# Strassen's scheme for up-projection pairs 2 to 18 in a one-core decoder layer

## The chip, the cores and the metric

The kernel runs on one core of a Trainium2 chip. The metric is the device time of one execution in microseconds (us). A run gives one time; the kernel before has three, and one further execution was taken with the hardware profiler, whose trace is read here. The core has a matrix engine (TensorE, PE in the profile, with its weight loads as PEld), VectorE (DVE), ScalarE (ACT), GpSimd (POOL) and SyncE (SP); SP and POOL here mostly issue DMAs.

## The reference

One layer of a decoder trunk on x of 512 positions by 1024 channels, float32. The changed part is the second half, the ConvGLU:

```python
h = rms_norm(x, g_ffn)
u = causal_depthwise_conv(h @ w_up, conv_w, conv_b)      # w_up: 1024 x 5632, conv of width 3
u_gate, u_val = split(u, 2)                              # 2816 columns each
x = x + (silu(u_gate) * u_val) @ w_down                  # w_down: 2816 x 1024
return rms_norm(x, g_final)
```

Ahead of it stand an RMS norm, the input projection, two attention branches of 8 heads, their gated merge (`g * (y @ W)` for two branches) and the output projection `m @ w_out` with the residual.

## The kernel before, in words

All products are done in the single-pass fp32r format with each operand split in a high part (a ScalarE copy to fp32r) and a low part (VectorE: value minus high part). One product is three matmuls, high by high, high by low, low by high (`mm3`, lines 90 to 92). Weights come from HBM into a raw tile of 128x1024 (five buffers, `wraw`), and the two parts go to rotating tiles, three for high parts and three for low parts (`wtile`).

The order of the PE instructions is the program's order. On the other engines a planner orders the instructions by a simulated time line, within the dependences and the explicit `issue_after` constraints, which say that an instruction stands behind another one.

The stages, in time order: input projection and attention; then the merge loop (`for i in range(KT)`), which for each of 8 blocks of 128 channels takes the gate projections from block 3 on and the two branch products with weight `ab`; the output projection, in Strassen form over 2x2 blocks; the residual, norm and transposes (`x1_root`, `x1_scale`, `x1_turn`, `x1_out`), which give `h2`, the normed activations, transposed, as 8 tiles of 128 channels by 512 positions in two parts; then the up-projection; then the down-projection, again in Strassen form, and the final norm.

The up-projection goes over 22 pairs. Pair i is columns 128i to 128i+127 of the gate half and of the value half of `w_up`. A plain pair (`plain`) takes two products of 1024 channels with 512 positions, 2 x 8 x 3 = 48 matmuls of 512 columns. The first two pairs, 0 and 1, are computed ahead in halves of 256 positions (`up_half`), the second half of the positions first, while the first half of the positions is still being transposed. A mixed pair treats the 2x2 blocks (channel half, gate or value) times (channel half, position half) by Strassen's scheme in seven block products of 4 x 3 = 12 matmuls of 256 columns, 84 in all (`first_four` has 48 of them: X, Q, Y, Z; `last_three` has 36). `MIXED` names the mixed pairs, 4 to 19. The PE order is first_four(i), last_three(i-1), first_four(i+1), and so on.

A mixed pair needs three things besides the plain ones:

- Sums of weights, made early by DMAs with addition between DRAM tensors (`sums_of`, tile `usum`, on POOL's DMA queue): per pair one copy of 1 MB, one addition of 512 KB and two additions of 256 KB.
- Split weights: `wa` (raw weights), `wb` and `wc` (sums), `wd` (half a tile), by `wmix`. For `wc` the low parts were computed during the merge loop (`split_ahead`: load the sum as `praw`, ACT and DVE split it, store the low part to DRAM as `ulo`) and are only loaded by SP (`wlo<-ulo`).
- Sums of activations (`mixes`): the four quadrants of `h2` in plain float32 are put into `h32` (two tiles, shown as `xa` in the trace) by 8 DMAs that copy the high parts and 8 DMAs that add the low parts (lines 1031 and 1033, POOL's queue); `mixes` makes four sums of 128x1024 on DVE (lines 965 to 968), and splits each with one ACT and one DVE instruction (lines 970 and 971) into `tm4`. `tm4[0]`, used by Y, is the first one that PE needs, then `tm4[2]` by Z, `tm4[1]` and `tm4[3]` by last_three.

After its products every pair goes through `glu`: the width-3 convolution (two ACT and four DVE instructions, lines 911 to 914), SiLU on ACT (917), the product (928), and after odd pairs the sums for the down-projection (576 to 579) and their split (337 and 338).

`step` (lines 665 and 666) makes a one-element copy on DVE and one on POOL, behind which the next part of a list of DMAs is issued; three such steps in `glu` belong to the weight sums of the down-projection (`dsums`).

Of the kernel before, what the change touches and what calls it, by code (L numbers as in the profile page):

```python
# [10 lines left out]
F32 = mybir.dt.float32  # L11
F32R = mybir.dt.float32r
# [15 lines left out]
NP = FT // 2  # L28
MIXED = range(4, 20)
SPILL = (1, 2, 3)  # L30
HOMES = (8, 10, 7)
DSUM = (0, 4, 5)
AHEAD = MIXED
NL = 3
# [12 lines left out]
def trunk_layer(ctx: ExitStack, tc: tile.TileContext, x: bass.AP, xT: bass.AP, w: bass.AP, vec: bass.AP,  # L47
# [223 lines left out]
    with tc.issue_after(nc.gpsimd.tensor_copy(small[:, 31:], r1[:, :1]).ins):  # L271
        for _ in quarter_sums("oi", list(enumerate(osum))):
            pass
        usum = {i: wdr.tile([4, 128, 512], F32, name=f"usum{i}") for i in MIXED}

        def sums_of(pairs, n=3):
            for group in (pairs[j:j + n] for j in range(0, len(pairs), n)):
                for i in group:
                    nc.gpsimd.dma_start(usum[i], flat(("ui", i, 0), 2), max_dma_last_dim=8192)
                for i in group:  # L280
                    adds(usum[i][0:2], flat(("ui", i, 2), 1))
                for i in group:
                    adds(usum[i][3], usum[i][0])
                for i in group:
                    adds(usum[i][2], usum[i][3])

        sums_of(MIXED)

# [301 lines left out]
    psp = pool(tst, "psp", 1)  # L590
    ulo = {i: wdr.tile([128, 2, 512], F32R, name=f"ulo{i}") for i in AHEAD}
    ahead = list(AHEAD)

    def both(q):
        return q.rearrange("h p c -> p h c")

    def split_ahead():
        if not ahead:
            return
        i = ahead.pop(0)  # L600
        raw = psp.tile([128, 2, 512], F32, name="praw", bufs=3)
        nc.gpsimd.dma_start(raw, both(usum[i][2:4]))
        with tc.issue_after(wload.hi.ins):
            nc.scalar.activation(phi, raw, AF.Copy)
        lo = raw.bitcast(F32R)
        with tc.issue_after(wload.lo.ins):
            nc.vector.tensor_sub(lo, raw, phi.bitcast(F32))
        nc.gpsimd.dma_start(ulo[i], lo)

    for i in range(KT):  # L610
        if i >= NG:
            fillers.append(gates(i, split_ahead))
            fill(1000)
        wab = wload(("ab", i))
        split_ahead()
        g = pend[i]
        for b, br in enumerate("ab"):
            ps = pmm.tile([128, S], F32, name="mm")
            for p in range(4):
                mm3(ps, blk(wab, b * 4 + p), (yhl[br, p][:, 0], yhl[br, p][:, 1]), p == 0, p == 3)  # L620
# [18 lines left out]
    x1s = pool(hst, "x1s", 1, side="right")  # L639
    h2 = [x1s.tile([128, 2, S], F32R, name=f"h2{k}") for k in range(KT)]  # L640
    ost = ExitStack()
# [14 lines left out]
    splits = []  # L656
    dsums = (step for q in dsum.items() for step in quarter_sums("di", [q]))
    marks = iter(list(range(16, 31)) + list(range(8)))

    def step(todo, src):  # L660
        c = next(marks, None)
        if c is None:
            return
        seen = small[:, c:c + 1]
        nc.vector.tensor_copy(seen, src)
        with tc.issue_after(nc.gpsimd.tensor_copy(seen, seen).ins):
            next(todo, None)

    def split_in(p, raw):
# [213 lines left out]
    up_half(ups[3], wup[3], 1)  # L883
    for n in range(4):
        up_half(ups[n], wup[n], 0)
# [20 lines left out]
    def glu(i, us):  # L906
# [17 lines left out]
        elif i // 2 not in xa:  # L924
            j = i // 2
            xa[j] = xtile(j if j < 7 else SPILL[j - 7] if j < NP - 1 else 9)
        j = i // 2
        split = a_side(i % 2, lambda dst: nc.vector.tensor_mul(dst, ua, ub), glu.tm, xa[j] if i % 2 else None, xb[j])
        if split and i >= FT - 3:
            return split  # L930
        if split:
            split()
            if j in SPILL:
# [4 lines left out]
                for h in range(2):  # L938
                    nc.gpsimd.dma_start(away["a", j][:, h], xa[j][:, h])
        if i < 3:  # L940
            step(dsums, xb[j][:, 0, :1] if i % 2 else glu.tm[:, 0, :1])
        return split
# [18 lines left out]
    def mixes():  # L961
        neg = cw[:, :, FT + MIXED[0]:FT + MIXED[-1] + 1]
        nc.vector.tensor_scalar(neg, neg, -1.0, None, op0=OP.mult)
        b11, b12, b21, b22 = (quad(h, T) for h in range(2) for T in range(2))
        nc.vector.tensor_sub(b11, b11, b12)
        nc.vector.tensor_sub(b12, b22, b12)
        nc.vector.scalar_tensor_tensor(b22, b11, -1.0, b22, op0=OP.mult, op1=OP.subtract)
        nc.vector.scalar_tensor_tensor(b21, b22, -1.0, b21, op0=OP.mult, op1=OP.subtract)
        for n, q in enumerate((b11, b22, b12, b21)):
            nc.scalar.activation(tm4[n][:, 0], q, AF.Copy)  # L970
            nc.vector.tensor_sub(tm4[n][:, 1], q, tm4[n][:, 0].bitcast(F32))

# [10 lines left out]
    def wmix(i, parts, n=1024, lo=None):  # L983
# [11 lines left out]
        return hi, wlo  # L995

    def first_four(i):
        wa = wmix(i, [(slice(0, 1024), w[WIDX["up", i, 0]])])
        wb = wmix(i, [(None, both(usum[i][0:2]))])
        ps1, ps2 = up_ps(), up_ps()  # L1000
        X, Q, Y, Z = ps1[:, :256], ps1[:, 256:], ps2[:, :256], ps2[:, 256:]
        quarter(X, wa, 0, rows_of(0, 0), True)
        quarter(Q, wa, 1, rows_of(1, 0), False)
        quarter(Y, wb, 1, mixed_rows(1), True)
        quarter(Z, wb, 0, mixed_rows(3), False)
        p1s, p5s, v = (tmp[i % 2][:, n] for n in range(3))
        nc.scalar.activation(p1s, X, AF.Copy)
        nc.scalar.activation(p5s, Y, AF.Copy)
        nc.vector.tensor_add(v, Z, p5s)
        return ps1, ps2, p1s, v  # L1010

    def last_three(i, ps1, ps2, p1s, v):
        X, Q, Y, Z = ps1[:, :256], ps1[:, 256:], ps2[:, :256], ps2[:, 256:]
        wc = wmix(i, [(None, both(usum[i][2:4]))], lo=ulo.get(i))
        wd = wmix(i, [(slice(0, 512), w[WIDX["up", i, 1]][:, 512:])], 512)
# [11 lines left out]

    for i in range(2):
        plain(i)
    for k in range(KT):  # L1030
        nc.gpsimd.dma_start(h32[k // 4][:, k % 4], h2[k][:, 0].bitcast(F32))
    for k in range(KT):
        nc.gpsimd.dma_start(h32[k // 4][:, k % 4], h2[k][:, 1].bitcast(F32), accum_op=OP.add)
    for i in range(2, MIXED[0]):
        if i == MIXED[0] - 1:
            mixes()
        plain(i)
    prev = None
    for i in MIXED:
        cur = i, *first_four(i)  # L1040
        if prev:
            last_three(*prev)
        prev = cur
# [229 lines left out]
```

## Time and profile before

| | |
|---|---|
| three runs | 701.58, 702.32, 702.64 us; median 702.32 us |
| the profiled execution | 701.36 us, of which 699.6 us are the span from the first to the last instruction |
| PE busy | 690.9 us (99%), 4460 matmuls |
| PEld / DVE / ACT / POOL busy | 604.3 / 573.7 / 404.3 / 123.8 us |
| DMA | 184.13 MB, 263 GB/s on average |

Times inside the trace count from the span's start. A matmul's row shows its start and a length that includes the pipeline's depth; so the distance of two starts is what a matmul costs, not its length. A line number is that of the kernel before.

### The profile page before, as it was taken

To read this page: it belongs to the slowest core of one execution; us is meant where nothing else is said; L and a number is where in the kernel's file an instruction comes from. 1 tells how busy PE (TensorE), PEld (TensorE's weight loads), DVE (VectorE), ACT (ScalarE), POOL (GpSimd) and SP (SyncE) were. 2 spreads that over 40 slices of the span, in tenths; PEclk is the share of its full clock that TensorE was granted. 3 is DMA by queue.
4 is the path that set the end of the run, shared out by engine and by line. 5 is a ranking of instruction groups with operands and counts; after the bars stand their busy time and mean duration, and the time that the engine had idled before them with its cause. 6 is when DMAs were issued, how large, how long until landed. Compare 5 with 4: busy or idle time off the path is not lost.

```text
span 699.6 us, 11729 instructions
## 1 busy us (share of the span) xinstructions
PE 690.9 (99%) x4460; PEld 604.3 (86%) x4460; DVE 573.7 (82%) x901; ACT 404.3 (58%) x607; POOL 123.8 (18%) x200
## 2 busy tenths in 40 slices
PE   9999999999999999999999999999999999999995
PEld 6888888979888888888889889999999988888884
DVE  7778858598694777586876899989999998878996
ACT  6435445455564455445576666777777764546854
POOL 1211122233542122112312410000000003200000
PEclk9999999999999999999999999999999999999999
DMA  8799999999999688787998968889777765867703
GB/s 313 277 339 368 358 353 238 240 237 246 228 266 291 230 294 273 270 270 273 350 340 290 208 176 300 291 306 326 250 240 250 261 220 199 311 209 249 265 0 121
DMA packets 57577, 184.13 MB, mean 263 GB/s; under 512 B 6640, under 2 KB 7408, under 8 KB 51632
## 3 DMA queue, kind: packets, MB, share of 16 engines
q1 hardware_dynamic: 41136, 105.18, 42.5%
q0 software_dynamic: 16096, 77.87, 39.8%
q8 instruction: 35, 0.57, 0.3%
q10 hardware_dynamic: 288, 0.33, 0.1%
q14 instruction: 22, 0.18, 0.1%
HBM read 162.64 MB, written 64.75 MB: 325 GB/s over the span
## 4 chain that ended last, share of the span: by engine, by line
PE 98%; DVE 1%; ACT 1%; DMA 1%; issue 0%; ACTq 0%
PE b L92 12%; PE b L90 12%; PE b L91 12%; PE mm L90 11%; PE mm L92 11%; PE mm L91 11%; PE c L91 5%; PE c L90 5%; PE c L92 5%; PE q L209 3%; PE tp L480 3%; PE tp L504 3%; PE sc L404 1%; PE sc L414 1%; PE v L91 1%; PE v L90 1%
## 5 line engine op out<-in xcount | busy, mean ns | idle before, releaser
L90 PE MATMUL b<-h,whi 128*128 128x256 f32 (+1 forms) x320 | 95.8, 299 | 0.0
L91 PE MATMUL b<-h,whi 128*128 128x256 f32 (+1 forms) x320 | 95.7, 299 | 0.0
L92 PE MATMUL b<-h,wlo 128*128 128x256 f32 (+1 forms) x320 | 95.7, 299 | 0.0
L90 PE MATMUL mm<-xg,whi 128*128 128x512 f32 x224 | 89.8, 401 | 0.0
L85 ACT ACTIVATE whi<-raw 128x1024 fp32r<-128x1024 f32 (+2 forms) x62 | 59.8, 975 | 51.4 <-PE mm L92 16.8
L92 PE MATMUL mm<-xg,wlo 128*128 128x512 f32 x224 | 87.4, 390 | 0.0
L91 PE MATMUL mm<-xg,whi 128*128 128x512 f32 x224 | 87.3, 390 | 0.0
L992 ACT ACTIVATE whi<-raw 128x1024 fp32r<-128x1024 f32 x64 | 61.1, 954 | 37.5 <-PE b L91 28.1
L86 DVE TENSOR_TENSOR wlo<-raw,whi 128x1024 fp32r<-128x1024 f32 (+2 forms) x62 | 68.6, 1115 | 12.9 <-ACT whi L85 12.6
L90 PE MATMUL b<-xa,whi 128*128 128x256 f32 x256 | 70.7, 276 | 0.0
L91 PE MATMUL b<-xa,whi 128*128 128x256 f32 x256 | 70.7, 276 | 0.0
L672 ACT ACTIVATE whi<-raw 128x1024 fp32r<-128x1024 f32 x45 | 46.8, 1052 | 31.9 <-DVE raw L690 11.8
L90 PEld LDWEIGHTS b<-h,whi 128*128 128x128 f32 x320 | 60.1, 188 | 2.5
L91 PEld LDWEIGHTS b<-h,whi 128*128 128x128 f32 x320 | 60.1, 188 | 2.5
L92 PEld LDWEIGHTS b<-h,wlo 128*128 128x128 f32 x320 | 60.1, 188 | 2.5
L672 DVE TENSOR_TENSOR wlo<-raw,whi 128x1024 fp32r<-128x1024 f32 x45 | 54.7, 1221 | 5.7 <-ACT whi L672 5.6
L92 PE MATMUL b<-xa,wlo 128*128 128x256 f32 x192 | 53.0, 276 | 0.0
L90 PEld LDWEIGHTS mm<-xg,whi 128*128 128x128 f32 x224 | 42.1, 188 | 9.9 <-issue 1.8
L92 PEld LDWEIGHTS mm<-xg,wlo 128*128 128x128 f32 x224 | 42.0, 188 | 9.0
L91 PEld LDWEIGHTS mm<-xg,whi 128*128 128x128 f32 x224 | 42.2, 188 | 7.9
L91 PEld LDWEIGHTS b<-xa,whi 128*128 128x128 f32 x256 | 48.1, 188 | 0.0
L90 PEld LDWEIGHTS b<-xa,whi 128*128 128x128 f32 x256 | 48.1, 188 | 0.0
(282 smaller groups left out, 1747.4 us busy)
## 6 DMA issues: line engine op xcount, KB each, us to landing
raw<-w SPq DMA_DIRECT2D x103, 512.0 KB, 5.8
usum<-w POOLq DMA_DIRECT2D x16, 1024.0 KB, 25.6
raw<-usum SPq DMA_DIRECT2D x32, 512.0 KB, 5.2
usum<-w POOLq DMA_DIRECT2D x16, 512.0 KB, 19.6
usum<-usum POOLq DMA_DIRECT2D x32, 256.0 KB, 12.0
praw<-usum POOLq DMA_DIRECT2D x16, 512.0 KB, 5.6
ulo<-praw POOLq DMA_DIRECT2D x16, 512.0 KB, 5.3
wlo<-ulo SPq DMA_DIRECT2D x32, 256.0 KB, 3.6
```

The lines of the kernel that those rows point to most:

```text
L85: wload.hi = nc.scalar.activation(hi[:, sl], raw[:, sl], AF.Copy)
L86: wload.lo = nc.vector.tensor_sub(lo[:, sl], raw[:, sl], hi[:, sl].bitcast(F32))
L90: nc.tensor.matmul(ps, a[0], b[0], start=start, stop=False, **kw)
L91: nc.tensor.matmul(ps, a[0], b[1], start=False, stop=False, **kw)
L92: nc.tensor.matmul(ps, a[1], b[0], start=False, stop=stop, **kw)
L209: nc.tensor.matmul(qk0[c], w0[i][:, (k % 2) * 512 + c * 128:(k % 2) * 512 + (c + 1) * 128], xg[k][:, j], start=(k == 0 and n == 0), stop=( ...
L404: nc.tensor.matmul(scs[h // 2][:, h % 2, o:o + n], Q[i][r0:r0 + 32, c, qt * 128:(qt + 1) * 128], K[i][r0:r0 + 32, d, :n], start=False, sto ...
L414: nc.tensor.matmul(sc[:, h, o:o + n], q[r0:r0 + 64, c, qt * 128:(qt + 1) * 128], k[r0:r0 + 64, d, :n], start=m == 0, stop=m == 2, skip_gro ...
L480: nc.tensor.transpose(tp[:, h, c:c + 128], a[:, h, c:c + 128], ident)
L504: nc.tensor.matmul(av[h * 64:(h + 1) * 64, j, qt * 128:(qt + 1) * 128], v[:, kb, (2 * p + h) * 64:(2 * p + h + 1) * 64], aT[p][:, h, o + k ...
L672: splits.append((nc.scalar.activation(hi, raw, AF.Copy), nc.vector.tensor_sub(lo, raw, hi.bitcast(F32))))
L992: nc.scalar.activation(hi[:, :n], raw[:, :n], AF.Copy)
```

## The change

- `MIXED` goes from pairs 4 to 19 to pairs 2 to 18: 17 mixed pairs, and five plain ones (0, 1, 19, 20, 21).
- `AHEAD`, the low parts computed in the merge loop, goes from `wc` of all 16 mixed pairs to `wc` of pairs 2 to 15 and `wb` of pairs 2 and 3, 16 pieces again. For pairs 16 to 18 `wc` is split by DVE when it is used. In the merge loop the pieces begin at block 1, not at block 0.
- `h32` no longer comes from DMAs. For the first half of the positions 8 ACT copies take it from the transposes' PSUM banks; for the second half two DVE additions of 128x1024 join the parts of `h2`, which is one tile now.
- `mixes` becomes a generator in the order `tm4[2]`, `tm4[0]`, `tm4[1]`, `tm4[3]`; signs are moved into the splits. The first `wa`'s split is put behind the first of these splits, `first_four(2)`'s copy of X and all of `first_four(3)` behind the second, the two remaining plain `glu`s (pairs 0 and 1) behind the third and the fourth.
- The four halves of `up_half` for the first positions go in the order 2, 0, 1, 3, not 0, 1, 2, 3.
- The three `dsums` steps stand before the sums of `glu`, and `sums_of` has become a generator that is run to its end at once.

```diff
-MIXED = range(4, 20)
+MIXED = range(2, 19)
-AHEAD = MIXED
+AHEAD = sorted([(i, 1) for i in MIXED[:14]] + [(i, 0) for i in MIXED[:2]], key=lambda q: (q[0], -q[1]))
...
-    ulo = {i: wdr.tile([128, 2, 512], F32R, name=f"ulo{i}") for i in AHEAD}
+    ulo = {(i, h): wdr.tile([128, 2, 512], F32R, name=f"ulo{i}{h}") for i, h in AHEAD}
...
         wab = wload(("ab", i))
-        split_ahead()
+        if i:
+            split_ahead()
...
-    for n in range(4):
+    for n in (2, 0, 1, 3):
         up_half(ups[n], wup[n], 0)
...
-        nc.vector.tensor_sub(b11, b11, b12)
-        nc.vector.tensor_sub(b12, b22, b12)
-        nc.vector.scalar_tensor_tensor(b22, b11, -1.0, b22, op0=OP.mult, op1=OP.subtract)
-        nc.vector.scalar_tensor_tensor(b21, b22, -1.0, b21, op0=OP.mult, op1=OP.subtract)
-        for n, q in enumerate((b11, b22, b12, b21)):
-            nc.scalar.activation(tm4[n][:, 0], q, AF.Copy)
-            nc.vector.tensor_sub(tm4[n][:, 1], q, tm4[n][:, 0].bitcast(F32))
+        def halve(n, q, sign=1.0):
+            hi, lo = tm4[n][:, 0], tm4[n][:, 1]
+            act = nc.scalar.activation(hi, q, AF.Copy, scale=sign)
+            return act.ins, nc.vector.scalar_tensor_tensor(lo, q, sign, hi.bitcast(F32), op0=OP.mult, op1=OP.subtract).ins
+
+        nc.vector.tensor_sub(b22, b22, b12)
+        yield halve(2, b22)
+        nc.vector.tensor_sub(b12, b11, b12)
+        yield halve(0, b12)
+        nc.vector.tensor_add(b11, b11, b22)
+        yield halve(1, b11, -1.0)
+        nc.vector.tensor_sub(b21, b11, b21)
+        yield halve(3, b21)
...
-        wa = wmix(i, [(slice(0, 1024), w[WIDX["up", i, 0]])])
-        wb = wmix(i, [(None, both(usum[i][0:2]))])
+        with behind(early if i == MIXED[0] else ()):
+            wa = wmix(i, [(slice(0, 1024), w[WIDX["up", i, 0]])])
+            wb = wmix(i, [(None, both(usum[i][0:2]))], lo=ulo.get((i, 0)))
...
-    for i in range(2):
-        plain(i)
-    for k in range(KT):
-        nc.gpsimd.dma_start(h32[k // 4][:, k % 4], h2[k][:, 0].bitcast(F32))
-    for k in range(KT):
-        nc.gpsimd.dma_start(h32[k // 4][:, k % 4], h2[k][:, 1].bitcast(F32), accum_op=OP.add)
-    for i in range(2, MIXED[0]):
-        if i == MIXED[0] - 1:
-            mixes()
-        plain(i)
+    for k in (0, 2, 1, 3, 4, 6, 5, 7):
+        src = turn_banks[0, k // 4][k % 4 // 2][:, k % 2 * 256:(k % 2 + 1) * 256]
+        nc.scalar.activation(h32[k // 4][:, k % 4, :256], src, AF.Copy, scale=gffn[:, k:k + 1])
+    for h in range(2):
+        nc.vector.tensor_add(quad(h, 1), *(h2all[:, 4 * h:4 * h + 4, c, 256:].bitcast(F32) for c in range(2)))
+    mixed_in = mixes()
+    early = next(mixed_in)
+    ready = next(mixed_in)
+    for i in range(MIXED[0]):
+        with behind(next(mixed_in, ())):
+            plain(i)
     prev = None
     for i in MIXED:
-        cur = i, *first_four(i)
+        with behind(ready if i == MIXED[0] + 1 else ()):
+            cur = i, *first_four(i)
```

More of the change, by code (lines that the diff above doesn't have):

```diff
@@ L279, in sums_of @@
                     nc.gpsimd.dma_start(usum[i], flat(("ui", i, 0), 2), max_dma_last_dim=8192)
+                yield
                 for i in group:
                     adds(usum[i][0:2], flat(("ui", i, 2), 1))
+                yield
                 for i in group:
                     adds(usum[i][3], usum[i][0])
+                yield
                 for i in group:
                     adds(usum[i][2], usum[i][3])
-        sums_of(MIXED)
+                yield
+        for _ in sums_of(MIXED):
+            pass
     mqkp = pool(ysta, "mqkp", 4, side="right")
@@ L595, in both, with step @@
         return q.rearrange("h p c -> p h c")
+    dsums = (step for q in dsum.items() for step in quarter_sums("di", [q]))
+    marks = iter(list(range(16, 31)) + list(range(8)))
+    def step(todo, src):
+        c = next(marks, None)
+        if c is None:
+            return
+        seen = small[:, c:c + 1]
+        nc.vector.tensor_copy(seen, src)
+        with tc.issue_after(nc.gpsimd.tensor_copy(seen, seen).ins):
+            next(todo, None)
     def split_ahead():
@@ L599, in split_ahead @@
             return
-        i = ahead.pop(0)
+        q = i, h = ahead.pop(0)
         raw = psp.tile([128, 2, 512], F32, name="praw", bufs=3)
-        nc.gpsimd.dma_start(raw, both(usum[i][2:4]))
+        nc.gpsimd.dma_start(raw, both(usum[i][2 * h:2 * h + 2]))
         with tc.issue_after(wload.hi.ins):
@@ L607, in split_ahead @@
             nc.vector.tensor_sub(lo, raw, phi.bitcast(F32))
-        nc.gpsimd.dma_start(ulo[i], lo)
+        nc.gpsimd.dma_start(ulo[q], lo)
     for i in range(KT):
@@ L639, in trunk_layer @@
     x1s = pool(hst, "x1s", 1, side="right")
-    h2 = [x1s.tile([128, 2, S], F32R, name=f"h2{k}") for k in range(KT)]
+    h2all = x1s.tile([128, KT, 2, S], F32R, name="h2")
+    h2 = [h2all[:, k] for k in range(KT)]
     ost = ExitStack()
@@ L656, in trunk_layer @@
     splits = []
[L657 to L667, printed above, removed]
     def split_in(p, raw):
@@ L927, in glu @@
         j = i // 2
+        if i < 3:
+            step(dsums, uc[0][:, :1])
         split = a_side(i % 2, lambda dst: nc.vector.tensor_mul(dst, ua, ub), glu.tm, xa[j] if i % 2 else None, xb[j])
@@ L939, in glu @@
                     nc.gpsimd.dma_start(away["a", j][:, h], xa[j][:, h])
-        if i < 3:
-            step(dsums, xb[j][:, 0, :1] if i % 2 else glu.tm[:, 0, :1])
         return split
@@ L995, in wmix, with behind @@
         return hi, wlo
+    def behind(ins):
+        st = ExitStack()
+        for q in ins:
+            st.enter_context(tc.issue_after(q))
+        return st
     def first_four(i):
-        wa = wmix(i, [(slice(0, 1024), w[WIDX["up", i, 0]])])
-        wb = wmix(i, [(None, both(usum[i][0:2]))])
+        with behind(early if i == MIXED[0] else ()):
+            wa = wmix(i, [(slice(0, 1024), w[WIDX["up", i, 0]])])
+            wb = wmix(i, [(None, both(usum[i][0:2]))], lo=ulo.get((i, 0)))
         ps1, ps2 = up_ps(), up_ps()
@@ L1006, in first_four @@
         p1s, p5s, v = (tmp[i % 2][:, n] for n in range(3))
-        nc.scalar.activation(p1s, X, AF.Copy)
+        with behind(ready if i == MIXED[0] else ()):
+            nc.scalar.activation(p1s, X, AF.Copy)
         nc.scalar.activation(p5s, Y, AF.Copy)
@@ L1013, in last_three @@
         X, Q, Y, Z = ps1[:, :256], ps1[:, 256:], ps2[:, :256], ps2[:, 256:]
-        wc = wmix(i, [(None, both(usum[i][2:4]))], lo=ulo.get(i))
+        wc = wmix(i, [(None, both(usum[i][2:4]))], lo=ulo.get((i, 1)))
         wd = wmix(i, [(slice(0, 512), w[WIDX["up", i, 1]][:, 512:])], 512)
```

## The prediction

> **What bounds the kernel now.** I read the page first: busy times, the 40 slices, the chain that ended last.
>
> ```profile
> span 699.6 us, 11729 instructions
> PE 690.9 (99%) x4460; PEld 604.3 (86%) x4460; DVE 573.7 (82%) x901; ACT 404.3 (58%) x607; POOL 123.8 (18%) x200
> PE   9999999999999999999999999999999999999995
> DVE  7778858598694777586876899989999998878996
> PEclk9999999999999999999999999999999999999999
> PE 98%; DVE 1%; ACT 1%; DMA 1%; issue 0%; ACTq 0%
> ```
>
> PE carries 98% of the chain at the full clock. DVE stands at nine tenths through the last third of the slices, where the mixed pairs are, so it is the engine that can become late next. A busy PE is not yet a dense one, so next came starts of matmuls at the borders of the up-projection, and the windows between them.
>
> ```profile
> 391.20 0.40 PE L90 MATMUL b<-h,whi 128*128 128x512 f32 x1
> 412.98 0.28 PE L90 MATMUL b<-h,whi 128*128 128x256 f32 x1
> 565.31 0.40 PE L90 MATMUL b<-h,whi 128*128 128x512 f32 x1
> ...
> 391.20:412.98 21.78, 21.78 (x98) 18.02 (x97) 19.58 (x30) 12.91 (x15) 6.75 (x10) 1.00 0.93 209
> 412.98:565.31 152.33, 152.33 (x1345) 152.32 (x1344) 144.94 (x226) 112.30 (x169) 4.39 (x8) 1.00 0.79 272
> 565.31:587.10 21.79, 21.79 (x99) 18.02 (x97) 20.46 (x33) 11.70 (x16) 2.85 (x5) 1.00 0.50 167
> ```
>
> In a window stand its length, then busy time and instructions of PE, PEld, DVE, ACT, POOL, the clock, the DMA share and GB/s. The first and the last window are two plain pairs each, the middle one the 16 mixed pairs. By the code a plain pair has 48 matmuls and a mixed pair 84 (counts here take in one or two that overlap a border). 21.78 / 96 = 226.9 ns per 512 columns, 152.33 / 1344 = 113.3 ns per 256: half to within 0.1 ns, so no stall hides in either stage. A plain pair is 10.89 us, a mixed one 9.52 us.
>
> **The change, part by part.** *One plain pair becomes mixed (17, not 16):* 10.89 - 9.52 = 1.37 us less on PE, which sets the end. This is the one sure term, since no stall is there to be removed.
>
> *The start of the mixed stage* moves ahead by two pairs. Pairs 0 and 1 have been computed in halves, so PE goes from the last half straight into X of pair 2, where it now begins pair 2 as a plain one, at 391.20. X and Q take 24 x 113.3 ns = 2.72 us, so Y needs `tm4[0]` at 393.92, Z needs `tm4[2]` at 395.28, the next X comes at 396.64 and last_three(2) at 402.08. What stands before that:
>
> ```profile
> 379.08 0.86 ACT L807 ACTIVATE h<-b,vecs 128x256 fp32r<-128x256 f32 x2 [0.21 <-DVE h L808]
> 382.96 1.06 ACT L85 ACTIVATE whi<-raw 128x1024 fp32r<-128x1024 f32 x1 [3.02 <-PE b L91]
> 385.68 1.06 ACT L85 ACTIVATE whi<-raw 128x1024 fp32r<-128x1024 f32 x1 [1.66 <-PE b L91]
> ...
> 375.54 1.23 DVE L828 TENSOR_TENSOR wlo<-raw,whi 128x1024 fp32r<-128x1024 f32 x1 [1.43 <-ACT whi L824]
> 379.58 0.88 DVE L808 SCALAR_TENSOR_TENSOR h<-b,vecs,h 128x256 fp32r<-128x256 f32 x2 [0.15 <-ACT h L807]
> 384.06 1.23 DVE L86 TENSOR_TENSOR wlo<-raw,whi 128x1024 fp32r<-128x1024 f32 x1 [3.59 <-ACT whi L85]
> 404.31 1.22 DVE L965 TENSOR_TENSOR xa<-xa 128x1024 f32<-128x1024 f32 x1
> 405.45 0.74 DVE L912 SCALAR_TENSOR_TENSOR t<-b,vecs,t 128x511 f32<-128x511 f32 x1
> ...
> L971 DVE TENSOR_TENSOR xa<-xa,xa x4: 1212/1214/1218, 406.9 to 420.7; 128x1024 fp32r<-128x1024 f32 x4
> L807 ACT ACTIVATE h<-b,vecs x16: 457/474/477, 364.8 to 379.5; 128x256 fp32r<-128x256 f32 x16
> 380.50:391.20 10.70, 10.70 (x96) 10.70 (x94) 5.65 (x7) 4.24 (x5) 5.07 (x7) 1.00 1.03 299
> ```
>
> ACT and DVE end the transposes' output at 379.94 and 380.46 and then idle 3.02 and 3.59 us; in the 10.7 us to 391.2 they work 4.24 and 5.65. The new chain goes there. ACT: eight copies of the form of line 807, 8 x 0.474 = 3.8 us, four of which are needed first. DVE: two additions, four sums and four low parts of 128x1024, ten of 1.22 us, 1.14 apart when dense (404.31 to 405.45), so 11.4 us; ACT's four high parts of 1.06 lie between. To Y go two additions, two sums, two low parts; with the low part of `wa` for pair 2 behind them that is seven: 380.46 + 7 x 1.14 = 388.4, 2.8 us before 391.20. The weight tile for this `wa` is free in time: before, the first two halves' weight tiles come free at 382.96 and 385.68 (what ACT waits for there), in the order 2, 0, 1, 3 one half later, 385.68 and about 388.4. If all ten and `wa` go first, PE waits: 380.46 + 11 x 1.22 = 393.9, 2.7 us late. Below nothing is excluded, as PE is dense from 377 on. I take 0, since the constraint behind the first split is what puts `wa` early; the end 2.7 stays for the range. The addition of the second half can begin earlier still, in the 1.43 us of idle before 375.54.
>
> The `glu` of pairs 0 and 1, behind the third and fourth split, is late by this, but its PSUM banks are wanted only by pair 4, at 406.2: nothing.
>
> *Low parts for `wb` of pairs 2 and 3 by DMA, `wc` of 16 to 18 on DVE.* The loads wait for a weight tile and stand in order on SP; raw loads behind them were issued pairs ahead.
>
> ```profile
> L991 SPq DMA_DIRECT2D wlo<-ulo x32: 320/415/1259, 418.6 to 555.3; - x32
> DMA to landing us min/median/max: 2.5/3.6/5.5
> 425.00:555.00 130.00, 130.00 (x1150) 130.00 (x1148) 123.91 (x196) 95.14 (x143) 4.39 (x8) 1.00 0.81 279
> L994 DVE TENSOR_TENSOR wlo<-raw,whi 128x1024 fp32r<-128x1024 f32 x28 | 34.1, 1217 | 1.3 <-ACT whi L992 1.3
> ```
>
> `wb` of pair 2 has a tile from 388.4 and is needed at 393.9, `wb` of 3 from 393.9 to 399.4, `wc` of 2 from 396.6 to 402.1: 5.5 us each, with a landing of 3.6 in the median and 5.5 at worst. Cost 0, at worst some 0.5 for the second issue; without this cover DVE would pay 1.22 a piece. On DVE a mixed pair costs 123.91 / 130 x 9.52 = 9.07 us of 9.52. Pairs 16 to 18 add 1.22: 10.3, 0.77 too much, 2.3 us behind after three. Pair i's PSUM sums have to be done only before last_three(i+2), 15 us after its own end, and then three plain pairs follow, not two, each with 48 matmuls to hide `glu` in. So 0; price without that cover, 2.3.
>
> *The POOL queue.* Four more DMAs for the 17th pair stand ahead of the first `praw`; 16 DMAs of `h32` go.
>
> ```profile
> 29.59 2.25 POOL L251 DMA_DIRECT2D osum<-w  x4
> 212.76 0.76 POOL L246 DMA_DIRECT2D usum<-usum  x1 [1.03 <-DMA usum<-usum]
> 214.22 0.77 POOL L602 DMA_DIRECT2D praw<-usum  x1 [0.70 <-DVE g L536]
> DMA to landing us min/median/max: 2.9/5.4/12.8
> 231.01 1.01 ACT L604 ACTIVATE spare<-praw 128x1024 fp32r<-128x1024 f32 x1
> 240.29 0.39 PE L90 MATMUL mm<-ya,whi 128*128 128x512 f32 x1
> ...
> 377.05 0.54 POOL L1031 DMA_DIRECT2D xa<-h  x1 [10.97 <-ACT h L807]
> 397.35 2.95 POOL L1033 DMA_DIRECT2D xa<-h  x3
> ```
>
> The 80 DMAs of both sums (5 x 16, 64 of `usum`, 16 of `osum`) take 29.59 to 212.76, 2.29 us each, so `praw` moves by 9.2, to land at 214.22 + 9.2 + 12.8 = 236.2. Beginning at block 1 moves its first use by one step of 24 matmuls, 5.44 us, to 236.45. What is queued behind it on ACT and DVE is the split of block 2's `ab` weights, needed by PE at 240.29: 236.2 + 1.0 + 1.06 + 1.22 = 239.5. Taken as 0; by the same row's median the load is 7 us early, and at worst a further 2 us of queueing would cost about 1.2. The last piece lies in slot 16 of 17, not of 18; the tiles that follow into its memory are wanted much later. `h32`'s DMAs, first row to last in the fence, gave DMA a share of 1.03 at 380 to 391; gone, they help SP's loads, and PE not at all. The moved `dsums` steps are as many as before: 0.
>
> **Sum.** 701.36 - 1.37 = 699.99 for the profiled execution, which stands 0.96 under the runs' median; on the median, 702.32 - 1.37 = 700.95. About 0.2% (1.4 us) is what a measurement of this kernel can tell from no change, and the forecast lies almost on that border.
>
> **The rivals.**
>
> A, *the start is late* (the other side): the first `wa` or `tm4[0]` comes after PE. It decides from 2.8 us of delay in the chain above, that is if the planner puts third and fourth split, or a `glu`, ahead of it. Price 2.7: 702.32 - 1.37 + 2.7 = 703.65; a convolution of pair 0 ahead of it as well, four instructions of 0.74, makes it 5.7 late, 706.6. Against it: the slack, and no PE stall in a stage where DVE is 95% busy.
>
> B, *DVE or a queue runs out of cover*, at pairs 16 to 18 (up to 2.3) or at the first `praw` (up to 1.2): 701.3 to 703.3.
>
> C, *more matmuls cost by their number*: a fixed part in each would eat into the saving, 36 of them. The two spacings above leave room for 0.1 ns each, 0.00 us; this has a chance of 0.03 for other tiles. The Trainium skill, "TensorE: Matmul & The Clock Gate", section "Wait — 56ns, not 53.3ns?", gives about 2.5 ns for each warm matmul on top of its columns; with that a mixed pair would be 84 x (2.5 + 112.2) = 9.63, the saving 1.26 and the time 701.06. By that rule the two spacings would differ from 2:1 by 2.5 ns; this trace has 0.1 and does not agree.
>
> D, *small delays go too*: PE has 0.37 us of lateness at the start of the down-projection,
>
> ```profile
> 591.63 0.39 PE L92 MATMUL c<-whi,xa 128*128 128x512 f32 x1
> 592.05 0.47 PE L90 MATMUL c<-whi,xa 128*128 128x512 f32 x1
> 592.36 0.40 PE L91 MATMUL c<-wlo,xa 128*128 128x512 f32 x1
> 603.94 0.49 PE L91 MATMUL c<-wlo,xa 128*128 128x512 f32 x1
> 604.27 0.40 PE L92 MATMUL c<-whi,xa 128*128 128x512 f32 x1
> ```
>
> three spacings of 0.42, 0.31 and 0.33 against 0.227. With three plain pairs ahead DVE may be on time there: 700.6.
>
> **How the numbers follow.** The forecast, 1.37 kept, 0.57 (own range 700.4 to 701.5: half of the three runs' spread of 1.06 us on either side); half of it falls beyond the border. D 0.13, faster. C 0.03, same. A 0.16: 0.13 slower, and 0.03 same where the lateness is about what PE saves. B 0.11, half of it same and half slower. So faster 0.42, same 0.40, slower 0.18. Range 700.2 to 703.5: D's lower end with the same spread, up to the nearer end of A; beyond lie A's worse part and little else.
>
> **What would show it.** After: 17 x 84 matmuls of 256 columns from about 391.2 to 553.1 without a wait, three plain pairs to 585.7, then the down-projection 1.37 us earlier. Wrong would be: PE idle before Y of pair 2 with DVE at `tm4`, idle near 240 with ACT at `praw`, or spacings over 113.3 ns in pairs 16 to 18.

## The result, and the profile after

| | before | after |
|---|---|---|
| median (22 runs each) | 702.27 us | 706.12 us |
| the profiled execution | 701.36 us, span 699.6 us | 702.12 us, span 700.4 us |

The ratio is 1.0053 (95% interval 1.0042 to 1.0063): the change makes the kernel 3.8 us slower, where 1.4 us of gain were forecast. One of the 22 runs of the kernel before, of 771.33 us, was in a slow state and does not count in the ratio (without it the median is 702.25). The changed kernel's time spreads from 701.79 to 709.24 us, and its profiled execution is among the quickest, so a second execution, of 706.39 us, is read beside it below ("the second execution").

The page of the changed kernel, the lines that answer to those of before:

```profile
span 700.4 us, 11800 instructions
PE 691.2 (99%) x4496; PEld 605.0 (86%) x4496; DVE 578.3 (83%) x909; ACT 409.0 (58%) x620; POOL 112.9 (16%) x188
...
PE   9999999999999999999999999999999999999995
...
PEclk9999999999999999999999999999999999999999
...
PE 95%; DVE 2%; DMA 1%; ACT 1%; issue 1%; ACTq 0%; DVEq 0%
```

There are 36 matmuls more, as there must be, and PE is still at 95% of the chain. The stages tell more. First the windows of the kernel before, from the first gate product of the merge loop on: merge loop, first half of the output projection, the halves of pairs 0 and 1, and pair 2 to the down-projection.

```profile
225.20:327.33 102.13, 102.13 (x452) 84.59 (x451) 72.72 (x89) 48.47 (x53) 19.75 (x33) 1.00 0.80 265
327.33:349.09 21.76, 21.76 (x97) 18.02 (x96) 19.35 (x33) 12.51 (x16) 8.88 (x16) 1.00 1.02 360
367.19:391.20 24.01, 24.01 (x210) 24.01 (x208) 16.57 (x33) 14.41 (x29) 7.80 (x12) 1.00 0.87 277
391.20:587.10 195.90, 195.90 (x1539) 188.38 (x1537) 184.98 (x287) 136.91 (x198) 13.98 (x23) 1.00 0.77 253
```

The same stages of the changed kernel, with the mixed pairs (392.88 to 554.72) by themselves as well:

```profile
225.54:327.68 102.14, 102.14 (x453) 84.60 (x452) 70.90 (x88) 47.68 (x53) 21.13 (x35) 1.00 0.82 268
327.68:349.65 21.97, 21.97 (x97) 17.94 (x96) 18.13 (x30) 12.21 (x15) 7.99 (x15) 1.00 1.00 370
368.62:392.88 24.26, 24.26 (x209) 24.25 (x208) 21.77 (x36) 19.11 (x40) 0.56 (x1) 1.00 0.50 184
392.88:587.47 194.59, 194.59 (x1575) 188.79 (x1573) 185.74 (x292) 137.46 (x203) 9.08 (x18) 1.00 0.74 252
...
392.88:554.72 161.84, 161.84 (x1430) 161.84 (x1429) 155.48 (x246) 120.17 (x181) 7.64 (x14) 1.00 0.80 273
```

The saving is there: 194.59 for 195.90 us, 1.31 less, and 161.84 / 17 = 9.52 us a mixed pair, as before. It is lost outside that stage: 0.34 by the start of the merge loop, where no changed instruction has run on PE, 0.21 and 0.87 in the two halves of the output projection (0.56 of it in one wait of PE at 351.74), 0.25 in the halves of pairs 0 and 1, and 0.4 after the up-projection. The second execution, near the median, shows more of what a usual run holds. Its chain of waits, by engine:

```profile
PE 54%; DMA 21%; issue 17%; POOL 4%; DVE 2%; ACT 1%; SPq 0%; POOLq 0%; ACTq 0%
```

and its windows, first the merge loop and the first half of the output projection, then two parts of the merge loop, then the halves of pairs 0 and 1 and the stage from pair 2 on:

```profile
225.44:331.72 106.28, 104.40 (x452) 85.53 (x451) 70.03 (x87) 46.95 (x52) 21.76 (x36) 0.98 0.82 258
331.72:355.01 23.29, 22.06 (x97) 17.94 (x96) 19.82 (x33) 12.61 (x16) 7.34 (x15) 1.00 1.01 375
...
311.00:314.61 3.61, 1.73 (x7) 0.78 (x5) 2.91 (x3) 2.06 (x3) 0.00 (x0) 1.00 0.91 288
314.61:318.02 3.41, 3.41 (x10) 2.67 (x9) 2.88 (x3) 2.09 (x3) 1.84 (x3) 0.50 0.78 171
...
373.15:397.74 24.59, 24.58 (x210) 24.36 (x209) 21.93 (x37) 19.43 (x41) 0.56 (x1) 1.00 0.51 178
397.74:592.33 194.59, 194.59 (x1575) 188.79 (x1574) 185.73 (x292) 137.46 (x203) 9.06 (x18) 1.00 0.75 252
```

The chain that ended last runs no longer along PE alone: 21% of it is DMA and 17% issue. The merge loop takes 106.28 us, 4.15 more than before, and the output projection's first half 1.53 more. These two are 5.7 us; with the 0.24 of a later start and 0.58 in the halves of pairs 0 and 1, less the 1.31 saved, they come to 5.2 us, and the spans (704.7 and 699.6 us) are 5.1 apart. Near the end of the merge loop PE stands twice, and then runs at half clock for 3.41 us. What stands before it there, first on PE, then on ACT, then on DVE:

```profile
311.02 0.39 PE L92 MATMUL mm<-yb,wlo 128*128 128x512 f32 x1
312.58 0.50 PE L90 MATMUL mm<-xg,whi 128*128 128x512 f32 x1 [1.17 <-ACT whi L85]
...
314.03 0.50 PE L92 MATMUL mm<-xg,wlo 128*128 128x512 f32 x1 [0.72 <-DVE wlo L86]
```

```profile
307.87 1.03 ACT L621 ACTIVATE spare<-praw 128x1024 fp32r<-128x1024 f32 x1 [4.75 <-DMA praw<-usum]
310.52 1.06 ACT L342 ACTIVATE oa<-tm 128x1024 fp32r<-128x1024 f32 x1 [1.62 <-DVE tm L583]
311.49 1.04 ACT L85 ACTIVATE whi<-raw 128x1024 fp32r<-128x1024 f32 x1
```

```profile
308.93 1.22 DVE L624 TENSOR_TENSOR praw<-praw,spare 128x1024 fp32r<-128x1024 f32 x1 [2.76 <-ACT spare L621]
310.07 0.42 DVE L583 TENSOR_TENSOR tm<-tm 128x256 f32<-128x256 f32 x1
...
312.76 1.22 DVE L86 TENSOR_TENSOR wlo<-raw,whi 128x1024 fp32r<-128x1024 f32 x1
```

To be read from the middle: ACT waits 4.75 us for a piece to land (`praw`), so DVE's low part of the piece is late, behind it the sums for `oa`, and behind these, on ACT and DVE, the split of the gate weights (lines 85 and 86) for which PE stands 1.17 and 0.72 us. It is not a piece that PE needs; what it needs is queued behind one.

### The profile page after: what moved, and what is told of

Its sections match the earlier page's. It is cut to its first block, busy times and chain, and to the rows that moved or that the text cites. A ratio compares the mean times of both kernels' runs of the same rounds, so it can differ in the third digit from the quotient of the medians.

```text
span 700.4 us, 11800 instructions
## 1 busy us (share of the span) xinstructions
PE 691.2 (99%) x4496; PEld 605.0 (86%) x4496; DVE 578.3 (83%) x909; ACT 409.0 (58%) x620; POOL 112.9 (16%) x188
## 4 chain that ended last, share of the span: by engine, by line
PE 95%; DVE 2%; DMA 1%; ACT 1%; issue 1%; ACTq 0%; DVEq 0%
PE b L90 12%; PE b L91 12%; PE b L92 12%; PE mm L90 11%; PE mm L92 11%; PE mm L91 11%; PE c L91 4%; PE c L92 4%; PE c L90 4%; PE q L209 3%; PE tp L485 3%; PE tp L509 3%; PE sc L409 1%; PE sc L419 1%; DMA raw<-w 1%
## 5 line engine op out<-in xcount | busy, mean ns | idle before, releaser
L91 PE MATMUL b<-h,whi 128*128 128x256 f32 (+1 forms) x316 | 93.0, 294 | 0.0
L90 PE MATMUL b<-h,whi 128*128 128x256 f32 (+1 forms) x316 | 92.9, 294 | 0.0
L92 PE MATMUL b<-h,wlo 128*128 128x256 f32 (+1 forms) x316 | 92.9, 294 | 0.0
L1006 ACT ACTIVATE whi<-raw 128x1024 fp32r<-128x1024 f32 x68 | 64.9, 955 | 41.1 <-PE b L91 30.1
L85 ACT ACTIVATE whi<-raw 128x1024 fp32r<-128x1024 f32 (+2 forms) x60 | 57.9, 973 | 44.1 <-PE mm L92 16.8
L90 PE MATMUL b<-xa,whi 128*128 128x256 f32 x272 | 75.1, 276 | 0.0
L91 PE MATMUL b<-xa,whi 128*128 128x256 f32 x272 | 75.1, 276 | 0.0
L86 DVE TENSOR_TENSOR wlo<-raw,whi 128x1024 fp32r<-128x1024 f32 (+2 forms) x60 | 66.1, 1110 | 5.6 <-ACT whi L85 5.3
L679 ACT ACTIVATE whi<-raw 128x1024 fp32r<-128x1024 f32 x45 | 46.5, 1050 | 26.6 <-DVE raw L697 12.2
L91 PEld LDWEIGHTS b<-h,whi 128*128 128x128 f32 x316 | 59.3, 188 | 1.9
L90 PEld LDWEIGHTS b<-h,whi 128*128 128x128 f32 x316 | 59.4, 188 | 1.9
L92 PE MATMUL b<-xa,wlo 128*128 128x256 f32 x204 | 56.3, 276 | 0.0
L90 PEld LDWEIGHTS b<-xa,whi 128*128 128x128 f32 x272 | 51.1, 188 | 0.0
L91 PEld LDWEIGHTS b<-xa,whi 128*128 128x128 f32 x272 | 51.1, 188 | 0.0
```

Of the source, the lines that this page charges most:

```text
L85: wload.hi = nc.scalar.activation(hi[:, sl], raw[:, sl], AF.Copy)
L86: wload.lo = nc.vector.tensor_sub(lo[:, sl], raw[:, sl], hi[:, sl].bitcast(F32))
L90: nc.tensor.matmul(ps, a[0], b[0], start=start, stop=False, **kw)
L91: nc.tensor.matmul(ps, a[0], b[1], start=False, stop=False, **kw)
L92: nc.tensor.matmul(ps, a[1], b[0], start=False, stop=stop, **kw)
L679: splits.append((nc.scalar.activation(hi, raw, AF.Copy), nc.vector.tensor_sub(lo, raw, hi.bitcast(F32))))
```

## The experiments

A short name for the four parts: the *pieces* are the low parts computed in the merge loop, each one a load (`praw`), an ACT and a DVE instruction, and a store (`ulo`). A *slot* is the place of one piece, 24 matmuls, 5.44 us. A ratio with its 95% interval is to the kernel before as it was measured beside that group of runs; its median was 702.34, 701.90, 702.30 and 702.27 us in the four groups below. Where medians of different groups are subtracted, some 0.4 us of the difference can be the groups'.

**First: where is the loss?** T1 says that the last piece is late at the output projection, T2 that the mixed stage starts late, T3 that the sums of the 17th pair make the first piece late.

*The changed kernel again* (the second execution is one of these runs).

> The changed kernel once more, for a profile of another execution. Its times lay between 701.8 and 709.2 us, and the execution profiled so far took 702.1, so most executions lose some 4 us more than the trace shows. Theory T1 (late low parts: the last praw of the merge loop, in slot 16 of 17, holds ACT and DVE in order, and the splits, the loads of x and the first up weights of the output projection come some 5 us later): the extra PE idle time stands between 327 and 382 us, before the transposes of the norm, in w4 or the first up halves. Rival T2 (the start of the mixed stage waits for the DMA of low parts or for tm4): it stands between 392 and 407 us. Rival T3 (the 17th pair's sums make the first praw late): it stands between 235 and 262 us. Time 702 to 709, median about 706.

Measured: 707.85 us, ratio 1.0079 [1.0051, 1.0107] to the kernel before. Its trace is the one shown above: the loss lies in the merge loop and the output projection, none at the start of the mixed stage; T2 falls. T3's place, 235 to 262 us, is not where PE waits either: it waits at 311 to 314.

*The pieces begin at block 0 again.*

```diff
-        if i:
-            split_ahead()
+        split_ahead()
```

> The changed kernel with the low parts beginning at block 0 of the merge loop again, as before: 16 pieces in 18 slots. T1: the last piece leaves the merge loop one slot earlier, the delay at the output projection goes, and the time is 700.5 to 702.5 with little spread. T2: as the changed kernel, about 706 and spread. T3: the first praw is then needed 5.4 us earlier than in the changed kernel while its sums are as late, so PE waits more, 707 to 711.

Measured: 706.60 us, 1.0058 [1.0042, 1.0074]. Undoing the later start changes nothing that can be told from noise; T3 had said 707 to 711. In its trace PE waits at 279, 280 and 314, in the merge loop, and for 0.63 us near 607, but not in the output projection. So T1, which has 1.5 us there in the second execution, is at most a part.

*The kernel before, with its pieces begun at block 1.*

```diff
-        split_ahead()
+        if i:
+            split_ahead()
```

> The kernel before with nothing but the low parts beginning one step later, at block 1: 16 pieces in 17 slots, with 16 pairs of sums. T1: the delay at the output projection appears without any of the other edits, 704 to 707. T2 and T3: as the kernel before, 702.3.

Measured: 702.88 us, 1.0008 [0.9997, 1.0020], no wait of PE in the merge loop. Beginning later costs nothing that can be told from zero as long as the pieces are on time.

*Fourteen pieces*, without `wc` of pairs 14 and 15, whose low parts DVE then makes at use.

```diff
-AHEAD = sorted([(i, 1) for i in MIXED[:14]] + [(i, 0) for i in MIXED[:2]], key=lambda q: (q[0], -q[1]))
+AHEAD = sorted([(i, 1) for i in MIXED[:12]] + [(i, 0) for i in MIXED[:2]], key=lambda q: (q[0], -q[1]))
```

> The changed kernel with 14 pieces of low parts instead of 16 (wc of pairs 2 to 13, wb of pairs 2 and 3; wc of 14 and 15 on DVE when used), still from block 1. T1: the last piece lies two slots earlier, in slot 14 of 17, so the delay at the output projection goes: 700.5 to 702.5; if DVE has no cover for two more pairs of 10.3 us against 9.5, up to 1.5 more. T2 and T3: as the changed kernel, about 706.

Measured: 704.91 us, 1.0039 [1.0026, 1.0052]. Two pieces fewer at the end give back 1.2 us in the median, with intervals that overlap; no wait is left in the output projection, and those of the merge loop stay, at 290 to 314. So T1 is a smaller part, and for the larger one T3's cause is left, the late sums, though not its place.

**Second: the sums and the queue.** U says that the whole chain of pieces is late from the 17th pair's sums on, and that ACT and DVE, in order, pass it to PE; V lays the loss to the other edits, W to the traffic of the sums whatever their order.

*The kernel before, with the sums of one more pair, which nothing reads*, ahead of its first piece.

```diff
+SUMS = range(3, 20)
...
-        sums_of(MIXED)
+        sums_of(SUMS)
```

> The kernel before, 16 mixed pairs 4 to 19, with the four DMAs of the sums of one more pair (pair 3, used by nothing) ahead on POOL's queue. Theory U (the 17th pair's sums make the first praw land some 8 to 10 us later, and as each piece's load waits for an earlier piece's store, the whole chain of 16 pieces runs late; ACT and DVE wait for a piece in order, ahead of the next weights' split, and PE waits in the merge loop): first praw lands at 235 to 239 and not 227, PE waits of some us between 235 and 330, 704 to 709. Rival V (something else in the change, the mixed start or the moved pieces, makes PE wait in the merge loop): 702.3, as the kernel before.

Measured: 707.34 us, 1.0060 [1.0037, 1.0082]. Four DMAs alone, without any other part of the change, cost 5.4 us in the median (four of the six runs stand at 707.2 to 708.3, two at 703.5). V falls: a loss of this size needs no other edit.

*The changed kernel, with another order on POOL's queue*: the load of a piece stands behind the store of the piece before last.

```diff
+        with tc.issue_after(stored[-2].ins) if len(stored) > 2 else ExitStack():
+            nc.gpsimd.dma_start(raw, both(usum[i][2 * h:2 * h + 2]))
...
+        stored.append(nc.gpsimd.dma_start(ulo[q], lo))
```

> The changed kernel with one constraint more in the merge loop: from the fourth piece on, POOL issues the load of piece k behind the store of piece k-2, so no ready store stands behind a load that waits for a buffer. Theory U: the first pieces are late as in the changed kernel, but the chain takes about 4.3 us a piece and not 5.5, catches up by 1 us a piece, and the PE waits after 275 us go: 700.5 to 702.5. Rival W (the lateness is DMA bandwidth, whatever the order): 705 to 707.

Measured: 700.88 us, 0.9986 [0.9978, 0.9995] to the kernel before: 5.2 us under the changed kernel's median (4.9 when each is held against the kernel before of its own group, 3.85 above it and 1.02 below). The gain of 1.02 has the forecast's 1.37 within its interval; that 700.88 is so near to the forecast's 700.95 is partly luck, as the kernel before stood at 701.90 in this group. POOL's queue in the changed kernel, with the like two rows of a third piece left out:

```profile
253.80 0.56 POOL L625 DMA_DIRECT2D ulo<-praw  x1
260.25 0.71 POOL L619 DMA_DIRECT2D praw<-usum  x1 [5.89 <-DMA ulo<-praw]
260.95 0.58 POOL L625 DMA_DIRECT2D ulo<-praw  x1
...
274.95 0.71 POOL L619 DMA_DIRECT2D praw<-usum  x1 [5.86 <-DMA ulo<-praw]
275.65 0.58 POOL L625 DMA_DIRECT2D ulo<-praw  x1
```

and with the new order:

```profile
253.28 0.56 POOL L627 DMA_DIRECT2D ulo<-praw  x1 [4.73 <-DVE praw L626]
253.95 0.72 POOL L621 DMA_DIRECT2D praw<-usum  x1
257.44 0.56 POOL L627 DMA_DIRECT2D ulo<-praw  x1 [2.76 <-DVE praw L626]
258.25 0.73 POOL L621 DMA_DIRECT2D praw<-usum  x1 [0.25 <-issue]
262.49 0.56 POOL L627 DMA_DIRECT2D ulo<-praw  x1 [3.52 <-DMA ulo<-praw]
263.18 0.72 POOL L621 DMA_DIRECT2D praw<-usum  x1
266.77 0.56 POOL L627 DMA_DIRECT2D ulo<-praw  x1 [2.86 <-DVE praw L626]
```

There are three buffers, so a load waits until the store of the piece three before it has landed. In the first fence the store of the next piece stands *behind* that load, though its data is ready, and waits with it: one store at a time is under way, and a piece takes a store's landing and a load's issue, 253.80 to 275.65 in three pieces, 7.28 us each, against a slot of 5.44. In the second fence the store goes first and the load mostly finds its buffer free: 253.28 to 266.77 in three pieces, 4.50 us each. These are stretches; the order on the old queue changes along the loop. Over all sixteen pieces the row of their splits on ACT tells the average, first and last start over 15 steps. The kernel before, the changed kernel, its second execution, and the new order:

```profile
L604 ACT ACTIVATE spare<-praw x16: 1006/1029/1030, 231.0 to 307.7; 128x1024 fp32r<-128x1024 f32 x16
L621 ACT ACTIVATE spare<-praw x16: 1029/1029/1030, 234.5 to 316.4; 128x1024 fp32r<-128x1024 f32 x16
L621 ACT ACTIVATE spare<-praw x16: 1029/1029/1030, 236.2 to 321.2; 128x1024 fp32r<-128x1024 f32 x16
L623 ACT ACTIVATE spare<-praw x16: 1006/1030/1032, 238.8 to 312.9; 128x1024 fp32r<-128x1024 f32 x16
```

That is 5.11, 5.46, 5.67 and 4.94 us a piece. Against a slot of 5.44 the changed kernel never makes up a delay, and with the new order it makes up 0.5 us with every piece, though its first piece is the latest of the four. What waited for whom, in all sixteen pieces, for the changed kernel (first two rows, by line) and then with the new order:

```profile
  POOL praw L619: 52.2, 13
  POOL ulo L625: 17.3, 4
```

```profile
  POOL ulo L627: 58.5, 16
  POOL praw L621: 3.0, 3
```

POOL waited 52.2 us ahead of loads, and with the new order 3.0; it now waits ahead of stores, for data. The windows of that kernel for merge loop, first half of the output projection, and pair 2 to the down-projection:

```profile
226.06:328.19 102.13, 102.13 (x452) 84.57 (x451) 72.24 (x89) 48.04 (x53) 22.04 (x36) 1.00 0.89 289
328.19:349.95 21.76, 21.76 (x97) 18.02 (x96) 19.34 (x33) 12.50 (x16) 9.11 (x15) 1.00 1.02 355
392.05:586.62 194.57, 194.57 (x1574) 188.81 (x1573) 185.75 (x292) 137.47 (x203) 9.10 (x18) 1.00 0.76 252
```

The first two are those of the kernel before to 0.00 us, the third is 1.33 shorter. Only the start, 226.06 for 225.20, differs; it lies in the first 92 matmuls and goes from 225.20 to 226.27 over the profiles of all kernels here, whatever their edit.

By the Trainium skill, "DMA: Bandwidth & Descriptors", section "Anatomy of one DMA — SWDGE (gpsimd) path", a DMA of this queue takes about 2.0 us and its bytes at 436 GB/s, by estimate 3.2 us for the 512 KB of a piece. By that, 3.2 and 0.7 for the load's issue, the old order would take an estimated 3.9 us a piece, less than the slot. The page of the changed kernel's profile has this for the stores, the last figure being the median from issue to landing:

```profile
ulo<-praw POOLq DMA_DIRECT2D x16, 512.0 KB, 5.6
```

The trace does not agree: a store takes 5.6 us, in a stage whose DMA share is 0.82, and 5.6 with 0.7 is longer than the slot. That the busy DMA engines are the reason for 5.6 is not shown.

*The changed kernel, with the sums of pair 18 made after the last store.*

```diff
-        for _ in sums_of(MIXED):
+        for _ in sums_of(MIXED[:-1]):
...
+    with tc.issue_after(last_store.ins):
+        for _ in sums_of(MIXED[-1:]):
+            pass
```

> The changed kernel with the sums of the last mixed pair, 18, issued behind the last piece's store, after the merge loop, and not ahead of the pieces. Theory U: first praw lands at 226 to 230 while its use is one step later than before; no PE wait in the merge loop; 700.4 to 701.8, the 1.37 us of the saved matmuls. Rival V: as the changed kernel, about 706.

Measured: 702.30 us, 1.0004 [0.9992, 1.0016], above the range that U gave. The first piece lands at 229.1 us and most of the loss comes back, but the time is 1.4 us above that with the order alone: from 231.2 to 316.8 the pieces take 5.71 us each, so the last one is as late as in the changed kernel, and PE waits 1.34 us at 331 in the output projection and 1.15 at 605. An early first piece alone does not keep the last one on time.

*The changed kernel with 16 mixed pairs, 2 to 17.*

```diff
-MIXED = range(2, 19)
+MIXED = range(2, 18)
```

> The changed kernel with 16 mixed pairs, 2 to 17, and plain 18 to 21: PE's matmuls as in the kernel before, all the other edits as in the changed one. Theory U: the sums on the queue are as many as before, so the chain is on time to within the one step: 702 to 703, as the kernel before. Rival V: 706 to 708, the changed kernel's waits and 1.37 us of matmuls.

Measured: 703.14 us, 1.0021 [1.0008, 1.0033]. With the 17th pair's sums goes most of the loss, as U has it, but the time is a little above U's 702 to 703: 1.2 us over the kernel before of its group (701.90) stay without them.

**Third: is the order a gain by itself?**

*The kernel before with the new order* (the same edit as above).

> The kernel before, with the load of each piece put behind the store of the piece before last on POOL's queue, nothing else. Theory U1 (the order matters only where the pieces are late): in the kernel before the first piece lands at 227.0 us, 10 us earlier than after the change, and no matmul waits in the merge loop, so there is nothing to gain: within 0.4 us of the kernel before, about 702. Rival U2 (the order is a gain by itself, whatever the number of pairs, and the 700.9 us of the changed kernel with this order owes it that, not the 17th mixed pair): 700.9 or below, a gain of 1 us or more.

Measured: 702.31 us, 0.9999 [0.9990, 1.0007]. No gain: the order is worth something only where the pieces are late, and the gain of 0.14% above is not the order's by itself; the stage of the mixed pairs, 1.33 us shorter there, holds it.

*The kernel before with the unused sums and the new order.*

> The kernel before with the unused sums of a 17th pair ahead of the first piece (707.34 us, 5.4 above the kernel before) and the same order on POOL's queue as in the run before this one. U1: the first piece stays late, landing near 238, but the pieces then take less than the 5.44 us of their slot, the lateness runs down, and the time is within 0.5 us of the kernel before, 701.5 to 702.7. U2 (late sums cost by themselves, through their traffic or the late landing of the first piece): 705 or more.

Measured: 704.90 us, 1.0033 [1.0020, 1.0045]. A miss for both: half of the 5.4 us comes back (2.6 are left). The first piece lands at 238.7 us for a slot that begins near 231, and PE still waits five times between 257 and 315, though the pieces' splits, 238.7 to 314.3, are 5.04 us apart.

*The changed kernel with the new order and late sums of pair 18* (both edits above).

> The changed kernel with the order on POOL's queue and with the sums of pair 18 made after the merge loop. Each alone gave 700.88 (order) and 702.30 us (late sums). U1: once the order lets the pieces catch up, the early landing adds nothing: 700.6 to 701.1. U2 (the landing of the first piece still costs 0.5 us or more): 700.4 or below.

Measured: 701.27 us, 0.9984 [0.9975, 0.9992]. This is just above U1's 701.1; the early landing adds nothing to the order.

*The changed kernel with the new order, pieces begun at block 0.*

> The changed kernel with the order on POOL's queue and the pieces begun at block 0 again, so that the first piece, landing near 238, is 10 us later than its place in the program, and not 3 us. U1: the pieces catch up all the same, but the splits of the weights of blocks 1 and 2 stand behind the first piece on ACT and DVE, needed by PE at 235 and 240: PE waits 1 to 4 us there and the time is 702 to 705; this is what beginning one step later is worth. U2 (where the pieces begin is worth nothing once the order is right): 700.6 to 701.2.

Measured: 703.58 us, 1.0021 [1.0008, 1.0034], with waits of PE at 257, 264 and 275; U1 has the time, but had put the waits at 235 and 240. With the order right, beginning one step later is worth 2.3 us (1.28 above the kernel before of its group, for 1.02 below).

**Fourth: is the rest the distance to the slot, or traffic?** W1 and W2 in the words below.

*The changed kernel with the new order, pieces begun at block 2.*

```diff
-        if i:
+        if i > 1:
             split_ahead()
```

> The changed kernel with the order on POOL's queue and the pieces begun at block 2, one step of 5.44 us later still. Theory W1 (what counts is how far the first piece lands behind its place in the program, and whether the queue then catches up): ACT waits for hardly any piece and the time is 700.5 to 701.2, like order and late sums together (701.27) or order alone (700.88), with no wait of PE in the merge loop. Rival W2 (the traffic of the sums costs by itself): no better than 700.9 and PE still waits in some of the blocks; a W3, that the last piece, now in the last slot, is late at the output projection, would give 701.5 or more.

Measured: 701.03 us, 0.9985 [0.9975, 0.9995]: W1's time and no wait of PE in the merge loop, but not its reason: ACT is idle ahead of pieces for 42.4 us in all, more than the 32.9 with pieces from block 1. In this profile no wait of PE in the merge loop follows from it. W3's late last piece does not show.

*The changed kernel with its own order, pieces begun at block 2.*

> The changed kernel with its old order on the queue and the pieces begun at block 2. W1: the first piece then lands about on time, so most of the 4 us go: 701 to 703, the rest of the loss being the old order, which lets a late load pass its delay on to the end. W2 (traffic): 705 to 707, as the changed kernel.

Measured: 715.67 us, 1.0185 [1.0157, 1.0213]. Both theories missed it, W1's range by 13 us and W2's by 9. Who waited before its loads and stores:

```profile
  POOL praw L619: 68.3, 13
  POOL ulo L625: 11.6, 2
```

With the pieces begun later, the planner puts the load ahead of the store from the fourth load on, where it did so load after load only from the seventh; from 244.1 to 287.3 us a piece takes 7.2 us, over all sixteen 6.14, and the last one is split on ACT at 328.9. Beside the run before it only the order on the queue was edited, and it is worth 14.6 us. A wait of 3.77 us in the output projection is followed by half clock here too:

```profile
336.20:340.50 4.30, 0.53 (x3) 0.24 (x2) 4.30 (x8) 2.17 (x3) 1.28 (x2) 0.89 1.01 385
340.50:346.00 5.50, 5.50 (x14) 4.24 (x15) 2.67 (x4) 2.19 (x3) 1.96 (x3) 0.50 1.05 406
```

*The kernel before with the unused sums, the new order, pieces begun at block 1.*

> The kernel before with the unused sums of a 17th pair, the order on the queue, and the pieces begun at block 1 and not at 0 (without this last: 704.90 us). W1: 701.7 to 702.7, the time of the kernel before; so that order and one step later pay for the sums together. W2: 704 or more.

Measured: 702.62 us, 1.0008 [0.9997, 1.0019]. W1 holds here: above the kernel before of their own groups, the three runs (sums alone, with the order, with both) stand at 5.4, 2.6 and 0.35 us, so order (2.8) and one step later (2.3) pay for the 17th pair's sums together; W2, a price of the traffic itself, falls.

## Why the prediction was wrong

*The bound and the saving: right.* 1.37 us were forecast, 1.31 came in the changed kernel and 1.33 with the new order, at the same 9.52 us a mixed pair; rival C, a price for each matmul, would have made it 9.63 and did not come.

*The start of the mixed stage: right.* PE does not wait at Y or Z of pair 2, in this profile or in the second execution's; rival A did not come. The halves of pairs 0 and 1 take 0.25 us more, without a wait in the records. That is not explained.

*Low parts of `wb` and `wc`: right.* The 17 pairs are dense with DVE at 155.48 of 161.84 us.

*The 16 DMAs of `h32`: right.* The DMA share between 368 and 393 falls from 0.87 to 0.50, and PE has nothing from it.

*Rival D*: the delays near 591 and 604 did not go. PE's wait near 604 is 0.22 us in the changed kernel's profile, where the stage from the down-projection on is 0.4 us longer, and 1.15 and 1.24 in two of its variants. It has not been followed up; whether the moved `dsums` steps (taken as 0) have a part in it stays open.

*The POOL queue: this step failed.* Its arithmetic held: `praw` was to land at 236.2 us, and it landed at 234.5 and 236.2 in the two executions. The kind of wait held too, the splits queued behind `praw`, rival B's second half, but not its place: PE was to be idle near 240, and it waits at 311 to 314 in the second execution and between 279 and 328 in the variants that keep the old order. What failed is the price, "Taken as 0", and "at worst a further 2 us of queueing would cost about 1.2". It was worked out for the first piece, against block 2's weights at 240.29. The fifteen others were not looked at, but for the last one's slot, "16 of 17", which takes it for granted that a piece takes one slot.

The rows that could have warned are those of the kernel before's own queue, a store's time to landing and POOL's waits ahead of loads:

```profile
ulo<-praw POOLq DMA_DIRECT2D x16, 512.0 KB, 5.3
  POOL praw L602: 39.9, 12
```

Twelve loads wait there for the landing of an earlier store. A store's landing of 5.3 us and 0.7 for the load's issue behind it are 6.0 us, more than the slot's 5.44, wherever one store at a time is under way. In the kernel before this is so for some of the pieces only: on average they are 5.11 us apart, the first lands at 227.0 for its use at 231.01, and PE does not wait. The four DMAs put 7.5 to 9.2 us on the landing and the later block 5.44 on the use, which leaves a lead of 0 to 2 us, and the pieces are then 5.46 to 5.67 us apart. So a delay that a slack of 0.8 us was to take up was not taken up once but handed on for 80 us, and it reached PE far behind the first piece. Lead and order both count. With the new order the changed kernel loses nothing with a first piece at 238.8, later than its use. With pieces from block 0 and the 17th pair's sums, the kernel before loses 2.6 us in spite of the new order, as the first piece is then 7 us behind. The price is 5.2 us in the medians (706.12 for 700.88), or 4.9 with each held against the kernel before of its group. In the second execution some 1.7 us of the loss is the clock: 3.41 us at half speed.

*The sum*: with the order mended the kernel gains 1.02 us of the 1.37 forecast, within what the interval allows. The mistake was a queue's, not PE's. The range, which ended at 703.5, gave the first piece up to 1.2 us and had no term for the other fifteen.

Not settled are why the 16-pair version of the change still loses 1.2 us, and how much of the spread of single runs is the clock's.

## What to carry to other kernels

A stage with rotating buffers has a period of its own: work it out (a store's landing, what stands behind it on the queue, the load) and hold it against the period of the consumer. If it is as long or longer, a delay at the first element is not absorbed but carried to the end; if it is only a little shorter, the consumer can have waited before the delay is made up. So look at the lead over all elements, not at the first one alone. On an in-order queue put what is ready, here the store, ahead of what has to wait; here the planner, left to itself, chose worse when the pieces began later.

## What the runs showed of the hardware

In the second execution, after two gaps of 1.17 and 0.72 us, PE busy 1.73 of 3.61 us, the granted clock was 0.50 for 3.41 us: eight matmuls of 512 columns at 0.427 us each where 0.227 is usual, some 1.6 to 1.7 us of loss behind 1.9 us of waiting. The Trainium skill, "TensorE: Matmul & The Clock Gate", section "What's actually happening", has a window of 3413 ns and half rate after an idle one; the 3.41 us agree with it. Its section "Why this matters for your kernels" asks for gaps of no more than about 3 us; the second execution has none of that length and loses the clock all the same. Such gaps do not always cost the clock. In the kernel before with the unused sums, gaps of 1.40 and 0.72 us, ahead of 280.96 and 282.41, were followed by a clock of 1.00 from 283.0 to 286.5. What decides between the two is not shown. After the wait of 3.77 us with pieces from block 2, matmuls keep 0.427 us from 340.85 to 346.38, which is longer than one such window.
